# Softmax with a relative-position bias on Trainium2: the last rows that GpSimd scatters, dealt to the DMA engines by four transfers of 16 rows in place of three

## The chip, the cores and the metric

The kernel runs on one core of one Trainium2 chip. The metric is the device time of one execution in microseconds (us), and a version is judged by the median of several executions. The core has compute engines that each follow their own instruction stream (of them this kernel uses VectorE, ScalarE and GpSimd; the profile calls them DVE, ACT and POOL), a SyncE (SP) that only issues transfers and waits, and 16 DMA engines that move data between the chip's memory and the on-chip SBUF of 128 partitions.

## What is computed

The input is a tensor of logits of shape (2, 8, 2112, 2112) and a table of biases by head and clipped distance. A bias is added that depends only on `i - j` clipped to ±16, and a softmax over the last axis follows.

```
rel_clipped = np.clip(rel, -max_rel, max_rel) + max_rel
bias = rel_bias[:, rel_clipped].copy()
logits = logits + bias[None, :, :, :]
logits = logits - logits.max(axis=-1, keepdims=True)
exp = np.exp(logits)
return (exp / exp.sum(axis=-1, keepdims=True)).astype(np.float32)
```

Each of the 33,792 rows has 2112 float32 numbers, 8,448 bytes. 285.5 MB are read and as many are written.

## The kernel before

**Tiling.** Each of the 128 partitions owns 264 consecutive rows (`ROWS`). They are worked in 44 blocks (`N`) of six rows (`R`), and four buffers `X[0]` to `X[3]` hold one block each: 128 partitions by six rows, so 50,688 bytes a partition. VectorE adds the bias and finds the maximum of a row (line 250), ScalarE takes the exponential and its sum (line 259), VectorE multiplies by the reciprocal of the sum (line 271), all in place in the buffer.

**The main queue.** SyncE issues, on one hardware queue (q1 in the profile), a load of a block (line 106) and a store of a block (line 110) in turn, each as one transfer over all 128 partitions. A load into a buffer waits for the store that empties it. Each of the 16 DMA engines has the same number of partitions in such a transfer, eight.

**Three transfers that are cut up.** The first block's rows 0 and 1 and the third-last block's rows 3 to 5 are not stored by one transfer. Half of the partitions of these pieces, 32 to 95 (and in the first block some of 0 to 31), are stored by SyncE in small transfers (`parts`, line 290, with the tables `AHEAD` and `BEHIND`). The other partitions are stored by GpSimd with indirect transfers on a second queue that software fills (q0; `pieces`, line 165). For the third-last block, `BEHIND` is four transfers of 16 partitions each, and GpSimd stores partitions 0 to 31 and 96 to 127. There a piece is three rows of a partition: 3 x 2112 x 4 = 25,344 bytes.

**A plan.** GpSimd's transfers are described by a list of tuples `(n, p0, lap, keep)`. One tuple is one indirect transfer of `n` rows. Its row `i` reads partition `p0 + lap * i` of the buffer and writes to the block of the output whose number stands in a column of `sel`. `choose` (lines 150 and 156) fills that column: an `iota` writes the right block numbers, and then a chain of `affine_select` instructions replaces the number by `FAR`, past the end of the output, in every row that isn't in `keep`. Such a row is out of bounds, and the transfer drops it. So `keep` says which rows of a transfer carry a piece. An assertion makes sure that the tables together name each partition once.

**The order of the end.** GpSimd issues the first plan's transfers, makes the columns of the last plan at once, and then waits (lines 180 to 183) until SyncE reports that the third-last block is scaled (line 308). SyncE then issues the store of that block's first three rows (line 310), the four transfers of `BEHIND`, the store of the second-last block (line 312) and the two halves of the last block (lines 313 and 314), each when its rows are scaled. It waits for the buffers' semaphores, for GpSimd's transfers (line 317) and for the last two stores (line 318), and the kernel ends.

Of the kernel before, what the change touches and what calls it, by code (L numbers as in the profile page):

```python
# [15 lines left out]
def kernel(  # L16
# [36 lines left out]
    LAST = [  # L53
        (80, 0, 1, []),
        (48, 80, 1, list(range(16, 48))),
# [3 lines left out]
    ]  # L59
    FAR = 1 << 20  # L60
    for own, plan in ((AHEAD, FIRST), (BEHIND, LAST)):
# [287 lines left out]
```

## Time and profile before

| what | value |
|---|---|
| time, median of 3 runs | 1328.71 us (1326.79 to 1329.11) |
| the profiled execution's own span | 1327.4 us |
| VectorE busy | 977.7 us (74%) |
| ScalarE busy | 575.2 us (43%) |
| GpSimd busy | 56.6 us (4%) |
| bytes moved | 571.01 MB at a mean of 430 GB/s |

The span runs from the first to the last instruction. Queue rows of the profile list packets, megabytes, and the time of the packets as a share of 16 engines' time. A view of stretches lists, for each stretch of the span, the busy time of each engine, the DMA engines' share and the rate in GB/s; both count a packet where it starts. In a stretch as short as one packet, rate times length divided by the packet's size is therefore the number of DMA engines that began a packet in it.

### The profile page before, as it was taken

How to read it: one execution, taken by the hardware profiler on the slowest of the kernel's cores; microseconds unless marked ns; L12 is line 12 of the kernel's file. 1: busy time of each engine (PE TensorE's matmuls, PEld its weight loads, DVE VectorE, ACT ScalarE, POOL GpSimd, SP SyncE). 2: the span in 40 equal slices, each digit the busy share in tenths (PEclk: the TensorE clock that was granted, in tenths of full speed). 3: DMA queues.
4: the chain of work that ended last, by engine and by line, in shares of the span. 5: the costliest groups of instructions: out<-in, count | busy, mean ns of one | idle time of the engine just before them, and what ended most of it. 6: DMA issues, size and time to landing. Idle time of an engine off the chain costs nothing. (4 is left out here: it accounts for less than half of the span.)

```text
span 1327.4 us, 2638 instructions
## 1 busy us (share of the span) xinstructions
DVE 977.7 (74%) x917; ACT 575.2 (43%) x539; POOL 56.6 (4%) x90
## 2 busy tenths in 40 slices
DVE  7998667777877766787777767677877776687763
ACT  3474333444443343344444333444444343345431
POOL 2750000000000000000000000000000000000100
DMA  9999999999999999999999999999999999999998
GB/s 415 410 438 431 435 431 434 434 435 429 432 437 429 431 438 431 428 438 434 429 432 432 435 435 431 432 435 437 429 435 432 437 425 434 438 437 429 428 427 365
DMA packets 13564, 571.01 MB, mean 430 GB/s; under 512 B 1896, under 2 KB 1912, under 8 KB 1912
## 3 DMA queue, kind: packets, MB, share of 16 engines
q1 hardware_dynamic: 13112, 568.59, 99.3%
q0 software_dynamic: 416, 2.37, 0.4%
q14 instruction: 4, 0.03, 0.0%
q10 hardware_dynamic: 32, 0.02, 0.0%
HBM read 285.49 MB, written 288.92 MB: 433 GB/s over the span
## 5 line engine op out<-in xcount | busy, mean ns | idle before, releaser
L250 DVE CUSTOM_DVE_ANT_0 X<-X,F 128x2112 f32<-128x2112 f32 x264 | 605.2, 2354 | 307.2 <-DVEq L102 307.2
L259 ACT ACTIVATE X<-X,nmax 128x2112 f32<-128x2112 f32 x264 | 541.7, 2052 | 541.8 <-ACTq L102 520.1
L271 DVE TENSOR_SCALAR X<-X,rec 128x2112 f32<-128x2112 f32 x264 | 332.4, 1315 | 13.2 <-DVEq L102 0.2
L259 ACT ACT_TABLE_LOAD x11 | 14.1, 1283 | 184.3 <-ACTq L102 184.3
L165 POOL DMA_INDIRECT out_dram<-X,sel x10 | 13.7, 1366 | 1182.5 <-POOLq L102 1180.0
L259 ACT ACTIVATION_READ_ACCUMULATOR X<-X,nmax 128x1 f32 x264 | 49.2, 186 | 0.0
L156 POOL TENSOR_SCALAR_AFFINE_SELECT sel<-sel 128x1 int32<-128x1 int32 x64 | 40.5, 632 | 9.6 <-POOL sel L156 0.5
L244 DVE COPY F<-M 128x2135 f32 x11 | 26.1, 2374 | 0.5 <-DVEq L273 0.5
L250 DVE DVE_READ_ACCUMULATOR2_ANT nmax<- 128x1 f32 x264 | 21.6, 82 | 0.0
L267 DVE RECIPROCAL rec<-tot 128x3 f32<-128x3 f32 x88 | 14.9, 170 | 0.0
L206 DVE TENSOR_TENSOR F<-F 128x264 f32<-128x264 f32 x1 | 0.4, 433 | 7.0 <-DMA F<-in_rel_bias_dram 7.0
L150 POOL IOTA sel<- 128x1 int32 x10 | 2.4, 244 | 0.0
L236 DVE COPY M<-F 128x1848 f32<-128x1848 f32 x1 | 2.1, 2076 | 0.0
L125 DVE MEMSET F<- 128x264 f32 x1 | 0.3, 278 | 1.1 <-SPq L85 1.1
L210 DVE TENSOR_REDUCE F<-F 128x33 f32<-128x264 f32 x1 | 0.6, 606 | 0.0
L233 DVE TENSOR_TENSOR M<-F 128x264 f32<-128x264 f32 x1 | 0.4, 441 | 0.0
L225 DVE TENSOR_TENSOR F<-F,rbS 128x264 f32<-128x264 f32 x1 | 0.4, 428 | 0.0
L203 DVE TENSOR_SCALAR F<-F 128x8 f32<-128x8 f32 x4 | 0.4, 165 | 0.0
L238 DVE COPY M<-rbS 128x247 f32<-128x247 f32 x1 | 0.4, 405 | 0.0
L213 DVE STREAM_TRANSPOSE F<-F 128x64 f32<-128x64 f32 x1 | 0.2, 246 | 0.0
L218 DVE STREAM_TRANSPOSE F<-F 128x64 f32<-128x64 f32 x1 | 0.2, 245 | 0.0
L223 DVE TENSOR_SCALAR F<-F,rbS 128x8 f32<-128x8 f32 x1 | 0.2, 231 | 0.0
(18 smaller groups left out, 2.8 us busy)
## 6 DMA issues: line engine op xcount, KB each, us to landing
X<-in_logits_dram SPq DMA_DIRECT2D x44, 6336.0 KB, 44.6
out_dram<-X SPq DMA_DIRECT2D x41, 6336.0 KB, 52.6
out_dram<-X SPq DMA_DIRECT2D x3, 3168.0 KB, 19.2
out_dram<-X SPq DMA_DIRECT2D x1, 4224.0 KB
out_dram<-X SPq DMA_DIRECT2D x4, 396.0 KB, 48.5
out_dram<-X SPq DMA_DIRECT2D x4, 132.0 KB
out_dram<-X SPq DMA_DIRECT2D x1, 264.0 KB
out_dram<-X SPq DMA_DIRECT2D x1, 231.0 KB
```

Source lines behind the costliest of these rows:

```text
L150: step(g.iota(col, pattern=[[0, 1]], base=(p0 * ROWS + row) // unit, channel_multiplier=lap * ROWS // unit))
L156: step(g.affine_select(out=col, in_=col, pattern=[[0, 1]], base=base, channel_multiplier=mul, compare_op=op, fill=float(FAR)))
L165: g.indirect_dma_start(out=blocks, out_offset=bass.IndirectOffsetOnAxis(ap=sel[0:n, w : w + 1], axis=0), in_=bass.AP(tensor=x.tensor, offs ...
L203: then(v.tensor_scalar(out=m, in0=dp, scalar1=0.0, scalar2=None, op0=op))
L206: then(v.tensor_tensor(out=view(F, 0, [[W, H], [1, W]]), in0=view(F, 0, [[W, H], [1, W]]), in1=view(F, SC + 3 * PB, [[1, H], [0, W]]), op= ...
L210: then(v.tensor_reduce(out=F[:, RB : RB + W], in_=view(F, 0, [[1, W], [W, H]]), axis=mybir.AxisListType.X, op=ALU.add))
L236: then(v.tensor_copy(out=view(M, U + W, [[ROWS, PB], [1, ROWS - W]]), in_=view(F, SC + 7 * PB, [[1, PB], [0, ROWS - W]])))
L244: v.tensor_copy(out=F[:, :], in_=M[:, bass.ds(ROWS - STEP - j, FW)]).then_inc(dve, 1)
L250: v.tensor_tensor_reduce(out=x, in0=x, in1=F[:, STEP - 1 - r : STEP - 1 - r + S], scale=-1.0, scalar=BIG, op0=ALU.add, op1=ALU.min, accum_ ...
L259: nc.scalar.activation(out=x, in_=x, func=EXP, scale=-1.0, bias=nmax[:, r : r + 1], accum_out=tot[:, r : r + 1],).then_inc(expd, 1)
L267: v.reciprocal(out=rec[:, r0 : r0 + HALF], in_=tot[:, r0 : r0 + HALF]).then_inc(inv, 1)
L271: v.tensor_scalar_mul(out=x, in0=x, scalar1=rec[:, r : r + 1]).then_inc(scaled, 1)
```

## The change

In the last plan the first two transfers, which carry 32 pieces of partitions 96 to 127 (48 rows, of which 32 are kept) and none (80 rows, all dropped), stay as they are. The three transfers of 16 rows that carry partitions 0 to 31 become four, with other first partitions, with a step of one partition from row to row in all four, and with other rows kept.

```diff
     LAST = [
         (80, 0, 1, []),
         (48, 80, 1, list(range(16, 48))),
-        (16, 0, 2, [0, 1, 2, 3, 5, 6, 9, 10, 11, 12, 13, 14, 15]),
-        (16, 1, 2, [1, 2, 3, 5, 6, 8, 9, 10, 11, 12, 13, 14, 15]),
-        (16, 1, 1, [0, 7, 8, 13, 14, 15]),
+        (16, 0, 1, [0, 1, 2, 3, 4, 9, 14, 15]),
+        (16, 3, 1, [2, 3, 4, 5, 7, 8, 9, 10, 13, 15]),
+        (16, 11, 1, [10, 11, 12, 13, 14, 15]),
+        (16, 16, 1, [1, 3, 4, 11, 12, 13, 14, 15]),
     ]
```

In both versions the 16-row transfers keep 32 rows and so carry 32 pieces; before, 16 rows were dropped, now 32. Counted by the place in the transfer, places 0 to 15 carried 2, 2, 2, 2, 0, 2, 2, 1, 2, 2, 2, 2, 2, 3, 3, 3 pieces, and now carry 1, 2, 2, 3, 3, 1, 0, 1, 1, 2, 2, 2, 2, 3, 3, 4.

On GpSimd, before, the part of the stream from the third column of the last plan to the transfers reads as follows (`sel` is the table of block numbers, `X_59` the buffer of the third-last block; line 150 is the `iota`, 156 the selections, 165 the indirect transfer):

```order
L150 IOTA sel 128x1
L156 AFFINE_SELECT sel<-sel 128x1 x5
L150 IOTA sel 128x1
L156 AFFINE_SELECT sel<-sel 128x1 x4
L150 IOTA sel 128x1
L156 AFFINE_SELECT sel<-sel 128x1 x12
L165 DMA out_dram<-X_59,sel 11264x6336 x5
```

The same place of the changed kernel, whose lines stand one further down:

```order
L151 IOTA sel 128x1
L157 AFFINE_SELECT sel<-sel 128x1 x10
L151 IOTA sel 128x1
L157 AFFINE_SELECT sel<-sel 128x1 x6
L151 IOTA sel 128x1
L157 AFFINE_SELECT sel<-sel 128x1 x2
L151 IOTA sel 128x1
L157 AFFINE_SELECT sel<-sel 128x1 x9
L166 DMA out_dram<-X_59,sel 11264x6336 x6
```

Four columns in place of three are made, with 27 selections in place of 21, and six indirect transfers follow in place of five. Nothing moves on the other engines.

## The prediction

> **What bounds the kernel now.** I read the queue rows of the page first, then SyncE's waits, then stretches of the end. The page's DMA rows:
>
> ```profile
> DMA packets 13564, 571.01 MB, mean 430 GB/s; under 512 B 1896, under 2 KB 1912, under 8 KB 1912
> q1 hardware_dynamic: 13112, 568.59, 99.3%
> q0 software_dynamic: 416, 2.37, 0.4%
> ```
>
> The DMA engines are busy for the whole span, so the time is bytes divided by their rate, and only what leaves an engine empty can be won. The q0 row also tells what a dropped row costs in packets. The two plans together keep 44 + 64 = 108 rows and drop 36 + 112 = 148, and ten transfers that report once on each of 16 engines make 160: 416 in all. So a dropped row is still a (tiny) packet, and each transfer reports on every engine.
>
> What ended last is in SyncE's waits and in the last issues of SyncE and VectorE:
>
> ```profile
> SPq L318 <- DMA out_dram<-X: 13.9, 1, 13.9
> 1272.80 34.65 SPq L110 DMA_DIRECT2D out_dram<-X  x3
> 1285.23 2.36 DVE L250 CUSTOM_DVE_ANT_0 X<-X,F 128x2112 f32<-128x2112 f32 x1 [12.53 <-DVEq L102]
> 1303.25 3.78 DVE L271 TENSOR_SCALAR X<-X,rec 128x2112 f32<-128x2112 f32 x3
> ```
>
> The last store is issued at 1272.80 + 34.65 = 1307.45 us. The span of 1327.4 us ends some 20 us later, the last 13.9 of them in the wait for the last stores. In that time the engines only empty their queues. How they end shows in stretches of 0.94 us, the time of one half-block packet of 25,344 bytes:
>
> ```profile
> 1284.00:1303.10 19.10, 17.71 (x17) 12.89 (x12) 0.00 (x0) 1.00 1.01 434
> 1319.00:1319.93 0.93, 0.00 (x0) 0.00 (x0) 0.00 (x0) 1.00 1.01 436
> 1319.93:1320.87 0.94, 0.00 (x0) 0.00 (x0) 0.00 (x0) 1.00 0.94 404
> 1320.87:1321.81 0.94, 0.00 (x0) 0.00 (x0) 0.00 (x0) 1.00 0.88 377
> 1321.81:1322.74 0.93, 0.00 (x0) 0.00 (x0) 0.00 (x0) 1.00 0.57 245
> 1322.74:1323.68 0.94, 0.00 (x0) 0.00 (x0) 0.00 (x0) 1.00 0.56 243
> 1323.68:1324.62 0.94, 0.00 (x0) 0.00 (x0) 0.00 (x0) 1.00 0.25 108
> 1324.62:1325.55 0.93, 0.00 (x0) 0.00 (x0) 0.00 (x0) 1.00 0.13 55
> 1325.55:1326.49 0.94, 0.00 (x0) 0.00 (x0) 0.00 (x0) 1.00 0.00 0
> ```
>
> Rate times length over 25,344 bytes is the number of engines that begin a packet: 16, 15, 14, 9, 9, 4, 2, 0. Two engines work alone at the end. The sum is 69 packets, so dealt evenly they take 69 / 16 = 4.3 of these steps where now 7 are taken: (7 - 4.3) x 0.94 = 2.5 us, 0.19% of 1328.71, is all that any new dealing can win in this execution. The first row, in which only q1 moves, gives the price of a piece: 434 / 16 = 27.1 bytes a ns for an engine, so 25,344 bytes take 0.94 us.
>
> **Which engine is which.** No view prints the engine of a packet, but the trace has each packet's start and duration, and an engine's packets follow end to start within a few ns. Chained from the sixteen last reports backwards, with the order of sizes that SyncE's issues force, they fall into sixteen chains. The q0 packets in a chain (piece, dropped row or report) fit exactly one reading of the plan: row `i` of a 16-row transfer is on engine `i`, and of the 48 rows three in a row are on each engine. Engine 4, which by the plan has no piece at all, is the one chain without any. The last packet of each chain ends at (us):
>
> ```
> engine           pieces, old -> new    last packet ends
> 4                0 -> 3                1322.34
> 0                2 -> 1                1323.77
> 1, 2, 3          2, 2, 2 -> 2, 2, 3    1322.14, 1323.80, 1324.74 (order unknown)
> 5                4 -> 3                1324.92
> 7                4 -> 4                1323.74
> 8                5 -> 4                1325.90
> 6, 9 to 12       5 each -> 6 has 3     1320.85, 1321.23, 1321.85, 1324.45, 1325.94 (order unknown)
> 13, 14, 15       6 -> 6, 6, 7          1322.07, 1322.11, 1323.76 (order unknown)
> ```
>
> Of the five that can't be told apart, the one that ends at 1325.94 is at the same place of q1 as engines 5 and 7, which like engine 6 got nine pieces from the first block (9 to 12 got six or seven). I take it as engine 6, an estimate.
>
> **The change part by part.** *The pieces.* Five pieces of 0.94 us leave engines 0, 5, 6 (two) and 8, and five arrive on 3, 4 (three) and 15. The two that end last lose: engine 6 ends at 1325.94 - 1.87 = 1324.07, engine 8 at 1325.90 - 0.94 = 1324.96. Engine 4 becomes 1322.34 + 2.81 = 1325.15. Engine 3 becomes 1325.68 if it was the latest of its three, 1323.08 if the earliest (its first-block share, ten pieces against eleven on 1 and 2, speaks for the earliest). Engine 15 reaches 1324.70 at most. The new last one is therefore at 1325.15 to 1325.68, against 1325.94.
>
> A piece can cost more than its bytes, for engines stall while q0 is mixed in:
>
> ```profile
> 1244.00:1284.00 40.00, 21.50 (x20) 12.89 (x12) 4.26 (x5) 1.00 0.99 419
> q0 software_dynamic: 256, 1.62, 10.0%
> ```
>
> At 419 in place of 434 GB/s, 40 us lose 40 x 15 / 434 = 1.4 us on each engine. The second row is that of the stretch 1243 to 1284: 10.0% of 16 x 41 us is 65.6 us for 64 pieces, at most 1.02 us each, stalls of the packet itself included. With 1.02, engine 4 ends at 1322.34 + 3.06 = 1325.40. I take that: 1325.94 - 1325.40 = **0.5 us gained**. The bounds: nothing but the untouched engines left (1324.74), 1.2 us gained; and with twice the mean stall of 1.4 us on top of engine 4's clean 1325.15, since it takes the most pieces and had none, 1327.95, so 2.0 us lost.
>
> *More columns.* One `iota` and six selections more on GpSimd, made here:
>
> ```profile
> L156 POOL TENSOR_SCALAR_AFFINE_SELECT sel<-sel 128x1 int32<-128x1 int32 x64 | 40.5, 632 | 9.6 <-POOL sel L156 0.5
> 69.58 16.91 POOL L156 TENSOR_SCALAR_AFFINE_SELECT sel<-sel 128x1 int32<-128x1 int32 x12
> 1243.89 0.93 POOL L165 DMA_INDIRECT out_dram<-X,sel  x1 [1157.40 <-POOLq L102]
> 1248.63 0.85 POOL L165 DMA_INDIRECT out_dram<-X,sel  x1 [0.30 <-issue]
> ```
>
> 6 x 0.63 = 3.8 us, at the slow rate of the second row (16.91 / 12 = 1.4) 8.5 us, from 86.5 us on. GpSimd then idles for 1157 us, so this costs nothing; without that cover it would delay the transfers by as much.
>
> *One more transfer.* Its issue takes 0.85 + 0.30 = 1.15 us, after 1249.48 us. It adds 16 dropped rows and 16 reports, two tiny packets an engine. Taking all of 65.6 - 64 x 0.94 = 5.4 us for the 192 tiny packets there, one costs at most 0.03 us, so 0.06 us an engine: left out. The queue q0 alternates with q1 packet by packet, so it empties later:
>
> ```profile
> DMA to landing us min/median/max: 9.6/16.3/35.0
> ```
>
> The slowest transfer landed 35 us after its issue, at 1284 us. Two turns more with a 50,688-byte q1 packet (1.87 us each) make it 1288, far ahead of the end near 1326: hidden.
>
> *The last load.* VectorE's idle 12.53 us before 1285.23 is the wait for the last block's load, whose packets share the engines with these pieces. If an engine's load is late by x, so are VectorE and the last two stores. The earliest engine ends near 1320.9 and has sixteen packets of 0.94 us before that, so it reaches the first half-store at 1305.9 us; it is issued when the row at 1303.25 starts. Up to 2 us or so are thus covered, and behind that stands the earliest engine's own 5 us ahead of the last. Nothing.
>
> **The rivals.** *Neighbouring partitions collide (slower).* The new transfers step by one partition: engines 0 to 4 read partitions 0 to 4 in one transfer, engines 2 to 4 read 5 to 7 in the next, 12 to 15 read 28 to 31 in the last, at nearly the same time; the old ones stepped by two. If four such reads are served one after another, the last waits 3 x 0.94 = 2.8 us, and in the three-fold group 1.9 us. Engine 2, in both, would end at 1323.80 or 1324.74 plus up to 4.7, so 1328.5 to 1329.4; engine 4 at 1325.15 + 1.9 = 1327.0. That is 1.1 to 3.5 us slower, 1330 to 1332 us. It decides from 0.8 us of extra stall on engine 4. For it: the 1.4 us above show that pieces do stall something. Against it: that loss falls on all, and the old plan also read close pairs.
> [...]
>
> *More is won (faster).* The median run lies 1.3 us above the profiled span. If that excess sits on engines 6 and 8, which already end last, these give up 1.9 and 0.9 us there, and up to 2 us are won: 1326.7. More than the 2.5 us of an even deal can't be.
>
> *The pieces don't land as counted.* If rows fall on engines in another way than by the chains, or engine 6 isn't the late one, the end stays at 1325.94 or a late engine gets one more (1326.9): 1328.7 to 1329.7.
>
> **How the numbers follow.** The sum of 0.5 us gained was made on the profiled execution, whose span is 1.3 us under the median but inside the range of the runs. Taken off the median it gives 1328.71 - 0.5 = **1328.2 us**. About 0.2%, 2.7 us, is what a measurement of this kernel can tell from no change. The forecast (the late end is handed from engines 6 and 8 to engine 4) has 0.62, nearly all of it within 0.2%. The collision has 0.20, half of it beyond 0.2%; more won 0.10, of it 0.07 beyond; another landing 0.08, of it 0.03 beyond. Together: faster 0.10, same 0.76, slower 0.14. The range starts at 1326.0 (the even deal, 1328.71 - 2.5, rounded down) and ends at 1330.9, half way through the collision's 1.1 to 3.5 us; it also holds the spread of single runs.
>
> **What would show it.** After: q0 with 448 packets (108 + 164 + 176) and again 2.37 MB; six transfers at 1244 to 1251 us; the steps from 1322.74 on holding some nine engines, three to five, and at most one, where now 9, 4 and 2 stand; the last packet ending near 1325.4 for a span near 1326.9. The collision would show as a rate below 419 GB/s from 1264 to 1288 us and a tail past 1327. A last load that lands over 2 us later than 1285.2, or a gap in the tail before the half-stores, would make the prediction wrong in another way.

## The result and the profile after

The changed kernel takes 1347.23 us (1345.14 to 1349.04), the kernel before 1328.42 us in the same comparison: a ratio of 1.0141, 95% interval 1.0127 to 1.0155. That is 18.8 us slower, outside the predicted range and on the other side of the forecast. The profiled execution's span is 1345.5 us, against 1327.4.

The queue row of the page is as predicted, 448 packets and the same bytes:

```profile
q0 software_dynamic: 448, 2.37, 0.5%
```

The time is lost at the other end of the program. This is SyncE's issue of the second load into buffer 0, first of the kernel before and then of the changed one (start, duration, line):

```profile
86.97 0.37 SPq L106 DMA_DIRECT2D X<-in_logits_dram  x1
```

```profile
98.62 0.37 SPq L107 DMA_DIRECT2D X<-in_logits_dram  x1
```

It comes 98.62 - 86.97 = 11.65 us later. GpSimd's timeline of the changed kernel has the reason:

```profile
56.19 15.35 POOL L157 TENSOR_SCALAR_AFFINE_SELECT sel<-sel 128x1 int32<-128x1 int32 x10
81.91 16.23 POOL L157 TENSOR_SCALAR_AFFINE_SELECT sel<-sel 128x1 int32<-128x1 int32 x9
1257.24 0.94 POOL L166 DMA_INDIRECT out_dram<-X,sel  x1 [1159.10 <-POOLq L103]
```

The last selection ends at 81.91 + 16.23 = 98.14 us, before it ended at 69.58 + 16.91 = 86.49. In both versions the load is issued 0.48 us later. In the code the selections of `choose(LAST, ...)` (line 178 of the kernel before) stand ahead of `g.sem_inc(st[0], 16)` (line 182), with which GpSimd tells SyncE that buffer 0 is stored, since the pieces of the first block are its own transfers. SyncE takes that signal (line 305) before it issues the load. GpSimd's idle stretch of 1159 us begins only behind the signal. The account of the order of the end, above, has lines 180 to 183 as one wait for the third-last block; only line 183 is that wait, and lines 180 to 182 wait for the first block's stores and give this signal.

What the late load does to the DMA engines, in stretches of the changed kernel (the last two columns are the DMA engines' share and GB/s):

```profile
90.00:95.00 5.00, 5.00 (x5) 4.74 (x5) 4.71 (x3) 1.00 0.55 235
95.00:100.00 5.00, 4.85 (x7) 4.74 (x6) 2.85 (x3) 1.00 0.40 122
```

The engines run dry for about half of ten microseconds. Over the longer stretch that takes in what follows, the kernel before and then the changed one:

```profile
44.00:140.00 96.00, 84.76 (x79) 51.48 (x49) 38.49 (x32) 1.00 1.01 433
```

```profile
44.00:140.00 96.00, 84.67 (x79) 51.38 (x49) 49.04 (x40) 1.00 0.94 395
```

96 us at 395 in place of 433 GB/s are 96 x 38 / 433 = 8.4 us lost. That is less than half of 18.8. The rest shows in the tail of the changed kernel, VectorE's start on the last block, SyncE's last stores, and stretches from there:

```profile
1302.87 2.36 DVE L251 CUSTOM_DVE_ANT_0 X<-X,F 128x2112 f32<-128x2112 f32 x1 [16.79 <-DVEq L103]
```

```profile
1286.18 38.91 SPq L111 DMA_DIRECT2D out_dram<-X  x3
```

```profile
1311.00:1319.00 8.00, 7.85 (x9) 7.51 (x8) 0.00 (x0) 1.00 0.42 181
1319.00:1325.10 6.10, 5.51 (x6) 0.00 (x0) 0.00 (x0) 1.00 0.71 303
...
1336.70:1338.00 1.30, 0.00 (x0) 0.00 (x0) 0.00 (x0) 1.00 0.23 98
...
1342.00:1344.00 2.00, 0.00 (x0) 0.00 (x0) 0.00 (x0) 1.00 0.03 13
```

VectorE's wait for the last load ends at 1302.87, 17.6 us later than before (1285.23), and with it the last store is issued at 1325.09, 17.6 us later too. From 1311 us until then the engines are busy for 42% and then 71% of the time (181 and 303 GB/s), and at the end a few engines go on for 7 us beyond the rest. Before, the queues didn't run dry there: from 1285 to 1320 us the rate was 415 to 456 GB/s.

The trace's landings say which engines these are. Each of the 16 engines reports a load when its own share has landed; the list is how far each report lies behind the first (us), sorted, for three loads of each kernel:

```
before   107: 0.0 0.0 0.4 0.7 0.8 1.4 1.5 2.1 2.8 3.0 3.2 3.2 3.5 4.1 4.2 4.5
         407: 0.0 0.1 0.2 0.2 0.3 0.6 0.6 1.0 1.6 1.7 1.7 2.3 2.3 3.1 3.4 3.5
        1245: 0.0 0.0 0.0 0.1 0.1 0.3 1.4 1.7 3.4 3.6 3.6 4.1 5.3 5.3 5.4 5.5
after    117: 0.0 0.0 0.1 0.2 0.2 0.2 0.3 0.3 0.3 0.4 0.4 0.4 0.6 0.6 0.8 1.4
         416: 0.0 0.0 0.1 0.2 0.3 0.3 0.3 0.3 0.3 0.4 0.5 0.5 0.7 3.0 3.7 5.9
        1253: 0.0 0.0 0.1 0.2 0.2 0.2 0.3 0.3 0.3 0.4 0.5 0.5 6.1 8.6 9.3 11.0
```

Before, the engines are staggered over 4.5 us at 107 us, and they stay staggered, by 3.5 to 5.5 us. (The first block's unequal pieces may do that; no run tests it alone.) In the change they start in step after the dry stretch. Three are 3.0 to 5.9 us behind at 416 us, and four 6.1 to 11.0 us at 1253 us. Chaining the packets of the last 90 us as in the prediction, three of the four are engines 13, 14 and 15, which by the last plan have the most pieces (6, 6 and 7), and which before, with six pieces each, ended 4th, 5th and 9th of the 16 (1322.07, 1322.11 and 1323.76 us). Three engines' shares of the last load land 14 to 18 us behind the first engine's, and VectorE waits for them.

The landings also split the delay of the last load, trace against trace. At 1253 us the first engine's share of a load lands 7.9 us later than in the kernel before, the last engine's 13.4 us later; the last load is complete 17.6 us later. So 7.9 us are the loss at the front, 5.5 us the falling behind of the last engine up to there, and 4.2 us come with the last plan.

### The profile page after: what moved, and what is told of

It is laid out like the page before. It is cut to its first block, busy times and chain, and to the rows that moved or that the text cites. A ratio compares the mean times of both kernels' runs of the same rounds, so it can differ in the third digit from the quotient of the medians.

```text
span 1345.5 us, 2653 instructions
## 1 busy us (share of the span) xinstructions
DVE 977.8 (73%) x917; ACT 575.2 (43%) x539; POOL 68.6 (5%) x98
## 5 line engine op out<-in xcount | busy, mean ns | idle before, releaser
L251 DVE CUSTOM_DVE_ANT_0 X<-X,F 128x2112 f32<-128x2112 f32 x264 | 605.2, 2354 | 325.0 <-DVEq L103 325.0
L166 POOL DMA_INDIRECT out_dram<-X,sel x11 | 16.8, 1527 | 1184.0 <-POOLq L103 1181.3
L157 POOL TENSOR_SCALAR_AFFINE_SELECT sel<-sel 128x1 int32<-128x1 int32 x70 | 50.5, 721 | 10.5 <-POOL sel L157 0.5
```

What stands on the lines that cost most here:

```text
L157: step(g.affine_select(out=col, in_=col, pattern=[[0, 1]], base=base, channel_multiplier=mul, compare_op=op, fill=float(FAR)))
L166: g.indirect_dma_start(out=blocks, out_offset=bass.IndirectOffsetOnAxis(ap=sel[0:n, w : w + 1], axis=0), in_=bass.AP(tensor=x.tensor, offs ...
L251: v.tensor_tensor_reduce(out=x, in0=x, in1=F[:, STEP - 1 - r : STEP - 1 - r + S], scale=-1.0, scalar=BIG, op0=ALU.add, op1=ALU.min, accum_ ...
```

## The experiments

**The new deal with the signal first.** The line that makes the last plan's numbers, and the wait for them, go behind the signal:

```diff
-        choose(LAST, len(FIRST), Z1 - Z0, (N - 3) * R + Z0)
-        take(g, pool, made[0])
         take(g, main, 16 * (1 + len(AHEAD)))
         g.wait_ge(soft, 16 * len(FIRST))
         g.sem_inc(st[0], 16)
+        choose(LAST, len(FIRST), Z1 - Z0, (N - 3) * R + Z0)
+        take(g, pool, made[0])
         take(g, ready, 1)
```

> The changed kernel with the making of the last plan's block numbers moved behind the signal that releases the second load of the first buffer. Theory (the seven more GpSimd instructions hold that signal, and with it the load, back by 12 us): the load is issued near 87 us again or earlier, the DMA rate from 90 to 100 us is above 400 GB/s, and the time is within 3 us of 1328.4. Rival (the new deal of the pieces, or neighbouring partitions read at once, costs the time at the end): still 1342 to 1348.

1329.61 us against 1328.27, ratio 1.0011 (1.0001 to 1.0020). The load goes out at 81.78 us, and the tail is near the one that the prediction drew: in steps of 0.94 us from 1321.81 us, nine engines begin a packet, then six, three and one, where the prediction had some nine, three to five and at most one from 1322.74 us on:

```profile
81.78 0.37 SPq L107 DMA_DIRECT2D X<-in_logits_dram  x1
```

```profile
1321.81:1322.74 0.93, 0.00 (x0) 0.00 (x0) 0.00 (x0) 1.00 0.57 245
1322.74:1323.68 0.94, 0.00 (x0) 0.00 (x0) 0.00 (x0) 1.00 0.38 162
1323.68:1324.62 0.94, 0.00 (x0) 0.00 (x0) 0.00 (x0) 1.00 0.19 81
1324.62:1325.55 0.93, 0.00 (x0) 0.00 (x0) 0.00 (x0) 1.00 0.06 27
```

So 17.5 of the 18.8 us hang on where the last plan's selections stand, and at most some 2.7 us on the deal with its one more transfer.

**The old deal with the signal first**, the same move in the kernel before.

> The kernel before with the making of the last plan's block numbers moved behind the release of the load. Theory: the load comes somewhat earlier than at 87 us or at the same time; 1324 to 1329. Rival (the signal is not what the load waits for): the load stays at 87 us, 1328. It is also the other half of a comparison of the two deals without a late load.

1328.17 us, ratio 1.0000 (0.9991 to 1.0010), with the load at 81.79 us. The kernel before gains nothing from a load 5 us earlier: at 87 us the engines still have work queued (443 GB/s from 80 to 100 us). Beside the run above it says that the new deal alone is level or costs 0.1%.

**The old deal with more selections.** Four kernels add an `iota` and two, four, six or twelve selections to the kernel before, in a column that no transfer uses (here six):

```diff
-        choose(LAST, len(FIRST), Z1 - Z0, (N - 3) * R + Z0)
+        choose(LAST + [(16, 16, 1, [0, 5])], len(FIRST), Z1 - Z0, (N - 3) * R + Z0)
```

> The kernel before with one iota and six selections more, into a spare column that no transfer uses; its five transfers and its deal are the old ones. Theory (late signal): 1344 to 1349, the second load of the first buffer near 98 us. Rival (the deal costs it): 1327 to 1330, as before.

> The kernel before with one iota and two selections more, into a spare column. Theory (late signal): the load comes 3 to 4 us later, near 90.5 us, and the time is 1329 to 1336, between the two; a time of 1328 would say that the DMA engines have that much in hand at this point. Rival (the deal): 1328.

> The kernel before with one iota and four selections more in a spare column. Theory (late signal, with some time in hand): the load near 96 us and 1336 to 1342, between two selections (1332.6) and six (1344.8). A step, not a slope, would put it at one of the two.

> The kernel before with one iota and twelve selections more in a spare column. Theory: the load near 107 us. If the engines are in step already with six, each further us of delay costs one us: 1353 to 1355. If the cost keeps growing as from two to six selections (12 us for 5 us of delay): above 1360.

Six selections alone give 1344.84 us, ratio 1.0123 (1.0106 to 1.0140). The deal is the old one, so the rival falls. The stretch 44 to 140 us in the kernels with two, four, six and twelve, each fence one kernel:

```profile
44.00:140.00 96.00, 84.69 (x79) 51.39 (x49) 44.73 (x36) 1.00 0.99 417
```

```profile
44.00:140.00 96.00, 84.87 (x79) 51.58 (x49) 47.04 (x37) 1.00 0.96 405
```

```profile
44.00:140.00 96.00, 84.72 (x79) 51.42 (x49) 49.36 (x39) 1.00 0.94 395
```

```profile
44.00:140.00 96.00, 78.90 (x74) 51.13 (x49) 54.86 (x45) 1.00 0.88 370
```

Put together with the others: what is lost at the front is 96 x (433 - rate) / 433. The time is the median over that of the kernel before in the same comparison. Front and rest belong to the traced execution alone, so the rest is taken from it: its span, less the 1327.4 us of the trace before, less the loss at the front.

| kernel | load at, us | lost at the front, us | slower by, us | ratio (95%) | span longer by, us | rest, us |
|---|---|---|---|---|---|---|
| old, signal first | 81.8 | 0 | -0.1 | 1.0000 (0.9991 to 1.0010) | -1.6 | -1.6 |
| new, signal first | 81.8 | 0.4 | 1.3 | 1.0011 (1.0001 to 1.0020) | 0.5 | 0.1 |
| new, made early | 81.9 | 3.3 | 8.3 | 1.0062 (1.0042 to 1.0081) | 6.1 | 2.8 |
| old, two more | 93.7 | 3.5 | 4.3 | 1.0027 (1.0014 to 1.0040) | 5.4 | 1.9 |
| old, four more | 96.2 | 6.2 | 14.8 | 1.0111 (1.0091 to 1.0131) | 11.7 | 5.5 |
| old, six more | 98.7 | 8.4 | 16.6 | 1.0123 (1.0106 to 1.0140) | 16.0 | 7.6 |
| the change | 98.6 | 8.4 | 18.8 | 1.0141 (1.0127 to 1.0155) | 18.1 | 9.7 |
| old, twelve more | 105.0 | 14.0 | 20.6 | 1.0155 (1.0133 to 1.0176) | 19.3 | 5.3 |
| new, light deal | 99.9 | 10.2 | 15.4 | 1.0108 (1.0086 to 1.0130) | 15.1 | 4.9 |

From two to twelve selections the front's loss follows the load's delay. The rest doesn't: it grows from 1.9 us with two selections to 7.6 with six, and is 5.3 with twelve. Split by the landings as above, the last engine has fallen behind by 1.4, 2.8 and 0.9 us more than before with four, six and twelve selections, and by 5.5 in the change. The last plan then adds 4.1 to 4.6 us in all four, so the old deal pays there as much as the new one.

Two selections came out within the 1329 to 1336 us expected, four at the upper edge of its range. The load with two came at 93.7 us, not near 90.5: in the traced execution the second of the first block's transfers took GpSimd 3.81 us in place of 1.55 before the selections began. Its six runs spread from 1328.73 to 1334.68 us, and the traced one is the slowest. The guess for twelve (1353 to 1355, with the load near 107 us) failed. The load came at 105.0 us. At the front it lost 5.6 us more than six selections, about as a delay of 6.3 us should. But its last engine was 6.3 us behind the first when the last plan's pieces came, that of six 8.2, so the rest shrank.

**The change with a light deal for the late engines.** As many instructions on GpSimd as in the change, but two pieces each on engines 13 to 15, and four or five on the others:

```diff
-        (48, 80, 1, list(range(16, 48))),
-        (16, 0, 1, [0, 1, 2, 3, 4, 9, 14, 15]),
-        (16, 3, 1, [2, 3, 4, 5, 7, 8, 9, 10, 13, 15]),
-        (16, 11, 1, [10, 11, 12, 13, 14, 15]),
-        (16, 16, 1, [1, 3, 4, 11, 12, 13, 14, 15]),
+        (32, 96, 1, list(range(32))),
+        (16, 0, 1, list(range(13))),
+        (16, 13, 1, list(range(13))),
+        (16, 19, 1, list(range(7, 13))),
...
-        choose(LAST, len(FIRST), Z1 - Z0, (N - 3) * R + Z0)
+        choose(LAST + [(16, 16, 1, [0, 20])], len(FIRST), Z1 - Z0, (N - 3) * R + Z0)
```

> The changed kernel with as many instructions on GpSimd (31 selections, six iotas, one of the columns a spare that no transfer uses), so that the load is late as in the change, but with pieces dealt so that engines 13 to 15 get two each (with the change 6, 6 and 7) and the others four or five. Theory (the late load lets the engines fall into step, and the last plan's pieces then meet engines 13 to 15 as the late ones): the load near 98 us, the same loss from 90 to 100 us, but the end 3 to 6 us earlier than the change, 1341 to 1344. Rival (the tail is the bubble at the front alone, pushed through): 1346 to 1348.

1342.95 us, ratio 1.0108 (1.0086 to 1.0130). The front lost even more than in the change, and yet the end came 4.3 us sooner. The same stretch of the front, and the two before the last store's issue, with 406 and 337 GB/s where the change has 181 and 303:

```profile
44.00:140.00 96.00, 84.09 (x79) 51.45 (x49) 50.59 (x39) 1.00 0.92 387
```

```profile
1308.00:1316.00 8.00, 7.85 (x9) 7.52 (x8) 0.00 (x0) 1.00 0.94 406
1316.00:1322.10 6.10, 5.52 (x6) 0.00 (x0) 0.00 (x0) 1.00 0.79 337
```

The time lies in the expected range, but only in part for the expected reason. Split by the landings, the last engine has fallen behind by 2.7 us here and by 5.5 in the change, before the last plan begins, so that difference can't come from the deal. The last plan then adds 2.4 us here and 4.2 in the change. So 1.8 us are what the lighter deal for the late engines saves in these two traces. The falling behind itself remains: the last engine is 8.2 us behind the first at 1255 us.

**The numbers made early.** In the change, `choose(LAST, ...)` goes right behind `choose(FIRST, ...)`, ahead of the first transfers:

```diff
         choose(FIRST, 0, A1 - A0, A0)
+        choose(LAST, len(FIRST), Z1 - Z0, (N - 3) * R + Z0)
         take(g, pool, made[0])
...
-        choose(LAST, len(FIRST), Z1 - Z0, (N - 3) * R + Z0)
-        take(g, pool, made[0])
```

> The changed kernel with the last plan's block numbers made right after the first plan's, from 15 us on, ahead of the first transfers. Theory (only what stands between the landings and the release counts): the load near 82 to 87 us and 1327 to 1331, if the first transfers, now issued later than at 38 us since the selections are slow while VectorE adds, still land before that; if they land after 87 us, the load is late by as much and the time is up to 1345.

1335.90 us, ratio 1.0062 (1.0042 to 1.0081): a miss. The load was in time (81.93 us), but the first transfers went out at 57.06 in place of 37.72 us, and the stretch at the front has 418 GB/s:

```profile
57.06 1.40 POOL L166 DMA_INDIRECT out_dram<-X,sel  x1 [1.11 <-POOLq L103]
```

```profile
44.00:140.00 96.00, 84.66 (x79) 51.35 (x49) 20.45 (x12) 1.00 1.00 418
```

That is 3.3 us at the front. At 1246 us the last engine is only 0.6 us later than in the kernel before, but with the last plan the last load falls 5.7 us behind. One engine (11 or 12) reports the last store 4 us behind the next; in this trace its stalls from 1236 to 1300 us add up to some 5 us, and 21 of the 64 pieces take over 1.0 us, one 4.0 us. What brings these stalls wasn't tried.

No run was faster than the kernel before by more than its interval.

## Why the prediction was wrong

**The step that failed** is "*More columns*": "GpSimd then idles for 1157 us, so this costs nothing; without that cover it would delay the transfers by as much." The row quoted for it, with its idle 1157.40 us, is right, but the idle time begins after an instruction that takes 17 ns and stands in no row of the timeline: the signal of line 182. The prediction costed the selections against the transfers that need the numbers, and not against what is queued between the two on the same engine. Those six selections and the column they fill are nearly the whole cause: six added alone to the old kernel cost 16.6 us, and the change with all of the last plan's selections out of the signal's way gives back 17.5 of its 18.8.

**The size of that step** was fair as a duration and useless as a price. It was put at 8.5 us at the slow rate; the selections ended 11.65 us later. Of these, 2.2 us came ahead of them, since the second of the first block's transfers took GpSimd 3.82 us in place of 1.55, and 9.5 us are the longer stretch of selections itself (50.53 to 98.14 us, before 48.35 to 86.49). But a microsecond of delay has no fixed price. From 81.8 to 87 us it cost nothing; beyond 87 us, delays of 6.8, 9.2 and 11.7 us made the traced spans 5.4, 11.7 and 16.0 us longer.

**The hand-over of the end** took place, but not as a gain. With the signal first, a single engine begins a packet in the last step. Chained as before, it has three pieces, as engines 3 and 4 now have, and ends at 1325.86 us; the prediction took 1325.40 for engine 4. In the trace of the old deal with the signal first, engine 4, without a piece, ends at 1323.08 us and the last engine at 1324.33 us. Three pieces of 0.94 us put engine 4 at 1325.9, as found. So the deal made the end 1.5 us later by these two traces, and the gain of 0.5 us did not come. In the profile before, eight of the 64 pieces take over 1.0 us, with the old deal and the signal first one, and there engine 8 ends at 1323.24 in place of 1325.90 us. The late end that was to be handed over was in part the stalls of one execution, as far as one trace of each tells.

**The collision of neighbouring partitions** was named as the slower rival, with the right sign by accident. Long pieces did appear, but on engines that don't end last. The queue's row from 1243 to 1290 us and the stretch 1264 to 1288 us with the signal first, of the old deal and then of the new:

```profile
q0 software_dynamic: 256, 1.62, 8.3%
```

```profile
1264.00:1288.00 24.00, 13.21 (x13) 5.14 (x5) 0.00 (x0) 1.00 0.98 415
```

```profile
q0 software_dynamic: 288, 1.62, 9.8%
```

```profile
1264.00:1288.00 24.00, 12.36 (x13) 4.28 (x5) 0.00 (x0) 1.00 0.98 404
```

The same 64 pieces, with 32 tiny packets more, take 1.5% of 16 x 47 us longer, some 11 us in all, and 15 of the pieces take over 1.0 us. The pieces of partitions 0 to 3, begun between 1263.71 and 1264.64 us, take 2.52, 2.00, 1.38 and 1.14 us, those of 8, 10 and 11 from 1.8 to 2.9 us, where an undisturbed piece takes 0.94. So the rival's first sign, a rate below 419 GB/s, is there in part, though the profile before has 413 GB/s in that stretch too. Its second, a tail past 1327 us, is not. Engine 2 lost some 0.8 us on its two pieces, not up to 4.7, and engines 1 and 2 ended at 1323.6 and not at 1328; engine 4, which ended last, lost nothing. What the collision alone costs in time can't be told from these runs.

The reads of partitions 0 to 3 moved 4 x 25,344 bytes in the 3.45 us from 1263.71 to 1267.16 us, 29 GB/s together, where one engine alone moves 434 / 16 = 27.1 GB/s: about what reads served one after another would give. But in the old deal with the signal first, engines 0 and 1 read partitions 0 and 2 at overlapping times in 0.94 us each, and neither read was lengthened. The cause of the long pieces stays open.

**"More is won"** rested on a reading that doesn't hold: that the median run lies 1.3 us above the profiled span. In every run that has both, the time is 1.7 to 2.2 us longer than the span. A span of 1327.4 us therefore belongs to a time of 1329.1 to 1329.6 us, which is above the median.

**One more transfer, the tiny packets and the last load** cost nothing that can be seen in the run with the signal first: 448 packets, the last load taken up by VectorE at 1284.44 us. In the change itself the last load was late by 17.6 us, but for another reason than the one weighed.

## What to carry to other kernels

An engine's idle time covers more work only if nothing that others wait for stands between the work and the idle time: read the code in order from the added instruction to the next wait, and price every signal, also those without a row of their own. Put signals that release transfers ahead of work that isn't needed until later. And don't tune a deal of work among engines to the stagger of one trace: in these runs a dry stretch at 95 us put the engines in step (in the change within 1.4 us of each other at 117 us), other engines were the late ones at the end, and the pieces met them there.

## What the runs showed of the hardware

**Selections took longer beside VectorE's passes.** In the changed kernel the 70 selections, all of the same 128 numbers, take 185 ns at the least and 2137 at most. Two groups of the kernel with the new deal and the signal first, the first while VectorE works (3.65 of the 3.80 us from 99.60), the second while it stands idle (0.00 of the 2.80 us from 108.60):

```profile
99.61 3.87 POOL L157 TENSOR_SCALAR_AFFINE_SELECT sel<-sel 128x1 int32<-128x1 int32 x4
108.55 2.83 POOL L157 TENSOR_SCALAR_AFFINE_SELECT sel<-sel 128x1 int32<-128x1 int32 x9
```

That is 0.97 against 0.31 us each, and in the change the ten from 56.19 us took 1.5 each, with VectorE busy for 15.16 of 15.31 us. The longest selection, 2137 ns, is nearly as long as one of VectorE's passes over a row (2354 ns on average). What holds a selection up isn't shown.

**Engines that started in step didn't stay so.** Started in step, three engines were 3.0 to 5.9 us behind at 416 us and four up to 11.0 us at 1253 us, with the same bytes in every transfer. The staggered engines of the kernel before spread over 4.5 us at 107 us and over 5.5 us at 1245 us. By the chaining, in every kernel whose load came at 96 us or later, engines 13 to 15 were among the last when the last load arrived. Why these, and what slows them, stays open.
